# One plain feature tile fewer in each up product, and part of VectorE's preparation given to GpSimd

## The chip, the cores and the metric

The kernel runs on one core of a Trainium2 chip. A core has a matrix engine (TensorE, PE in the profile; PEld is its weight load), a vector engine (VectorE, DVE), an activation engine (ScalarE, ACT), a general engine (GpSimd, POOL) and a queue engine for transfers (SyncE, SP). Each runs its own instructions in order and waits for the others on semaphores. The metric is the device time of one launch in microseconds (us), here the median of several runs.

## The reference

One encoder layer over 512 tokens of 1024 channels, all in float32:

```python
def swiglu_ffn(x, w_gate, w_up, w_down):
    return (jax.nn.silu(x @ w_gate) * (x @ w_up)) @ w_down
...
x = x + 0.5 * swiglu_ffn(rmsnorm(x, ffn1_norm[l]), ffn1_w_gate[l], ffn1_w_up[l], ffn1_w_down[l])
x = x + hybrid_mixer(rmsnorm(x, mix_norm[l]), w_in[l], q_norm[l], k_norm[l], ...)
x = x + 0.5 * swiglu_ffn(rmsnorm(x, ffn2_norm[l]), ffn2_w_gate[l], ffn2_w_up[l], ffn2_w_down[l])
x = rmsnorm(x, final_norm[l])
```

The mixer (attention and pooling) lies between the two feed-forward blocks and isn't touched. A feed-forward block has 2816 features, 22 tiles of 128; each feature tile has a gate and an up column block.

## The kernel before, in words

**Numbers in two parts.** A float32 matmul operand is split into a high part (rounded by ScalarE) and a low part (the rest, a subtraction on VectorE, or a scaling and a subtraction). `split` does both, and `mm3` multiplies high by high, high by low and low by high: three matmuls for one product. So each operand, weights and activations, costs one ScalarE and one VectorE instruction before PE may use it.

**A plain feature tile.** Gate and up are each 8 blocks of 128 channels × 3 matmuls of 512 tokens, 48 matmuls. `evacuate` then multiplies the gate by the normalizer `norm.rb` (L424, from PSUM), applies SiLU on ScalarE (L426), multiplies by `norm.rb` again (L428) and has `down.place` multiply by the up product (L726, from PSUM). Every second tile is followed by two small operations on the stored result (L733, L734).

**A product tile.** The other feature tiles use a 2 × 2 block scheme with seven products in place of eight (Winograd's form): gate and up columns are the two columns of blocks of one operand, and channels and tokens are halved for the other. Seven products of 4 channel blocks × 3 matmuls of 256 tokens: 84 matmuls. The weight side needs per tile the parts of w11 (512 columns), the sums w13 and w24 (1024 each; L500, L506, L507) and w22 (1024), all with high parts at L477 and low parts at L482. The token side is made once for all product tiles, by `Norm.blocks`: eight scaled channel blocks (`scale`, L365), four sums of token blocks (`add`, L371: s1, s2, the sum in a21, s4), and seven split operands (L133 or L136): S2, S3, S4 as wholes of 1024 columns, and A11, A22, S1, A12 each as two halves of 512. In a product tile PE takes A11, S3, S2, A22, S1, A12, S4 in that order.

**The order.** `ffn_up` runs once for each feed-forward block. The first two feature tiles are multiplied together while the norm is finished; as soon as the normalizer is on the chip, the preparation by `Norm.blocks` may begin. Then come the remaining plain tiles, as many as `PLAIN` says for block 1 and block 2 (the two are counted in it), and the preparation is fed in between them by `piece`, from the list `todo`. The last plain tile also prepares the first product tile's weights. In the plain part a scheduler sets the order on each engine from its own estimates; only the transfers' queue keeps the order of the code. From the first product tile on the order of the code holds.

**GpSimd.** It issues the transfers that build sums of the down weights in memory (L717), a few after each feature tile, each group led by a one-column copy that holds it back (`mark`, L715); in the mixer it builds biases and trailing sums (L1221, L1430), and at the end of block 2 it multiplies by the last gain (L1808).

**Buffers.** Weight parts rotate through four places (three in `parts`, and `whi`/`wlo`). The halves `ha` take the buffers of the normalized input `hhi`/`hlo`, each free once PE's last plain tile has passed that channel block. `aside` holds the scaled blocks and sums.

Of the kernel before, what the change touches and what calls it, by code (L numbers as in the profile page):

```python
# [8 lines left out]
F32 = mybir.dt.float32  # L9
# [3 lines left out]
ALU = mybir.AluOpType  # L13
# [21 lines left out]
RAW = 2  # L35
HILO = 3
SHIFT = 16
PLAIN = (5, 4)
PROBS = 3
EARLY = 8  # L40
LATE = 12
# [15 lines left out]
def layer(  # L57
# [31 lines left out]
    nc = tc.nc  # L89
# [28 lines left out]
    A11, S1, S3, S2, A12, A22, S4 = range(7)  # L118
# [7 lines left out]
            what(*args)  # L126


    def split(src, hi, lo, scale=None):

        if scale is None:
            nc.scalar.copy(hi, src)  # L132
            nc.vector.tensor_tensor(lo, src, hi.bitcast(F32), op=ALU.subtract)  # L133
        else:
            nc.scalar.activation(hi, src, AF.Copy, scale=scale)
            nc.vector.scalar_tensor_tensor(  # L136
                lo, src, scale, hi.bitcast(F32), op0=ALU.mult, op1=ALU.subtract
            )
# [155 lines left out]
    class Norm:  # L294
# [5 lines left out]
        def add(self, k, square=True):  # L300
            hi = hpool.tile([P, S], F32R, tag="h", name=name("hhi"))
            lo = hpool.tile([P, S], F32R, tag="h", name=name("hlo"))
            split(x[k], hi, lo, gain_sb[:, self.which, k : k + 1])
            self.h[k] = hi, lo
            if square:
                self.square(k)
# [41 lines left out]
        def blocks(self, pool, aside):  # L348
# [7 lines left out]
            a11, a21 = x_lo[:, :, :HT], x_lo[:, :, HT:]  # L356
            a12, a22 = x_hi[:, :, :HT], x_hi[:, :, HT:]
            s2, s4, s1 = (
                z[:, at : at + 4 * HT].rearrange("p (k c) -> p k c", c=HT)
                for z, at in ((aside[0], 4 * S), (aside[1], 4 * S), (aside[2], 0))  # L360
            )
# [5 lines left out]
                    self.rb, op0=ALU.mult, op1=ALU.mult,  # L367
                )

            def add(dst, one, two, op):  # L370
                nc.vector.tensor_tensor(dst, one, two, op=op)  # L371

            def whole(i, src, make, sign=None):
                pair = [make().rearrange("p (k c) -> p k c", c=HT) for _ in range(2)]
                split(src, *pair, sign)
                self.a[i] = [[z[:, k] for k in range(4)] for z in pair]

            def halves(i, src):

                self.a[i] = [[], []]  # L380
                for k in (0, 2):
                    pair = [
                        hpool.tile([P, 2, HT], F32R, tag="h", name=name("ha")) for _ in range(2)
                    ]
                    split(src[:, k : k + 2], *pair)
                    for z, to in zip(pair, self.a[i]):
                        to.extend(z[:, j] for j in range(2))

            def by_x(i):
                return lambda: xpool.tile([P, 2 * S], F32R, tag=f"x{i.pop()}", name=name("xa"))  # L390

            def extra():
# [2 lines left out]

            free = [3, 2, 1, 0]
            return [(scale, k) for k in range(KD)] + [
                (add, s1, a21, a22, ALU.subtract),
                (add, s2, s1, a11, ALU.add),
                (add, a21, a11, a21, ALU.add),  # L400
                (whole, S3, a21, by_x(free), -1.0),
                (whole, S2, s2, by_x(free), -1.0),
                (add, s4, s2, a12, ALU.subtract),
                (whole, S4, s4, extra),
                (halves, A11, a11),
                (halves, A22, a22),
                (halves, S1, s1),
                (halves, A12, a12),
            ]


    def ffn_up(norm, wA, down, loaded, in_order, plain, turns=()):
# [9 lines left out]
        def evacuate(f, gate, up):  # L422
            g = temp()
            nc.vector.tensor_tensor(natural(g), ordered(gate), natural(norm.rb), op=ALU.mult)  # L424
            sg = temp()
            nc.scalar.activation(sg, g, AF.Silu)  # L426

            nc.vector.tensor_tensor(sg, sg, norm.rb, op=ALU.mult)  # L428
            down.place(f, ordered(up), sg)
            down.sums(f)  # L430
            return sg

        first = [bank() for _ in range(4)]
        for kp in range(KD // 2):
# [10 lines left out]
            for kk in range(2):  # L445
                k = 2 * kp + kk
# [1568 lines left out]
```

## Time and profile before

| what | value |
|---|---|
| median of 3 runs | 811.85 us (811.62 to 812.27) |
| the profiled execution | 811.69 us, span 809.7 us |
| PE busy | 797.8 us, 99% |
| VectorE busy | 712.8 us, 88% |
| ScalarE busy | 498.8 us, 62% |
| GpSimd busy | 147.2 us, 18% |
| mean granted clock of PE | 0.997 |

The span is counted from the first to the last instruction; the execution's own time holds about 2 us more around it. Times in the traces below start at the span's beginning. In a timeline row stand start, duration, engine, line, operation, out<-in and shape; idle time before it, and what ended it, in brackets. Neighbouring instructions of an engine overlap by some tens of nanoseconds, so what one costs its engine is read from start to start.

### The profile page before, as it was taken

How to read it: one execution, taken by the hardware profiler on the slowest of the kernel's cores; microseconds unless marked ns; L12 is line 12 of the kernel's file. 1: busy time of each engine (PE TensorE's matmuls, PEld its weight loads, DVE VectorE, ACT ScalarE, POOL GpSimd, SP SyncE). 2: the span in 40 equal slices, each digit the busy share in tenths (PEclk: the TensorE clock that was granted, in tenths of full speed). 3: DMA queues.
4: the chain of work that ended last, by engine and by line, in shares of the span. 5: the costliest groups of instructions: out<-in, count | busy, mean ns of one | idle time of the engine just before them, and what ended most of it. 6: DMA issues, size and time to landing. Idle time of an engine off the chain costs nothing.

```text
span 809.7 us, 14959 instructions
## 1 busy us (share of the span) xinstructions
PE 797.8 (99%) x5730; PEld 749.1 (93%) x5730; DVE 712.8 (88%) x1133; ACT 498.8 (62%) x854; POOL 147.2 (18%) x234
## 2 busy tenths in 40 slices
PE   9999999999999999999999999999999999999995
PEld 8889999999999999888888888899999999988985
DVE  7899999999996997778688788999999999987996
ACT  8446655556666665659659545465666655765683
POOL 0022212223220000100256354111111011100010
PEclk9999999999999999999999999999999999999998
DMA  8276889979999774431599777256666566969642
GB/s 289 76 208 208 237 226 247 216 189 249 248 292 316 220 219 147 142 124 34 156 258 248 196 198 210 80 112 204 172 184 151 163 185 168 272 210 344 211 120 104
DMA packets 73703, 158.56 MB, mean 196 GB/s; under 512 B 6544, under 2 KB 31648, under 8 KB 73248
## 3 DMA queue, kind: packets, MB, share of 16 engines
q1 hardware_dynamic: 49664, 109.09, 40.0%
q0 software_dynamic: 23680, 48.24, 28.3%
q8 instruction: 45, 0.74, 0.4%
q10 hardware_dynamic: 288, 0.27, 0.1%
q14 instruction: 26, 0.21, 0.1%
HBM read 153.38 MB, written 50.34 MB: 252 GB/s over the span
## 4 chain that ended last, share of the span: by engine, by line
PE 91%; DVE 4%; ACT 1%; issue 1%; DVEq 0%; ACTq 0%
PE mm L198 19%; PE mm L200 19%; PE mm L199 19%; PE a L199 10%; PE a L200 9%; PE a L198 9%; PE mm L1605 1%; PE mm L1516 1%; DVE aside L365 1%; PE a L1580 1%; PE mm L1580 1%; DVE aside L371 0%; PE a L1516 0%; DVE parts L133 0%; PE a L1605 0%
## 5 line engine op out<-in xcount | busy, mean ns | idle before, releaser
L571 ACT ACTIVATE t<-mm 128x256 f32<-128x256 f32 x105 | 40.5, 386 | 110.8 <-PE mm L200 108.8
L132 ACT CAST parts<-raw 128x1024 fp32r<-128x1024 f32 (+2 forms) x77 | 74.1, 968 | 54.7 <-PE mm L199 20.5
L133 DVE TENSOR_TENSOR parts<-raw,parts 128x1024 fp32r<-128x1024 f32 (+2 forms) x77 | 85.8, 1121 | 15.1 <-ACT parts L132 14.7
L199 PE MATMUL mm<-ha,parts 128*128 128x256 f32 x280 | 77.0, 275 | 0.0
L200 PE MATMUL mm<-ha,parts 128*128 128x256 f32 x280 | 77.0, 275 | 0.0
L198 PE MATMUL mm<-ha,parts 128*128 128x256 f32 x280 | 77.0, 275 | 0.0
L715 POOL COPY mark<-t 128x1 f32<-128x1 f32 x40 | 15.9, 397 | 330.9 <-DVE t L615 244.8
L717 POOL DMA_DIRECT2D wsum<-in_wB_dram x72 | 71.1, 1123 | 26.1 <-DMA wsum<-wsum 14.1
L482 DVE TENSOR_TENSOR parts<-wsum,parts 128x1024 fp32r<-128x1024 f32 x53 | 64.5, 1217 | 5.1 <-ACT parts L477 5.1
L477 ACT CAST parts<-wsum 128x1024 fp32r<-128x1024 f32 x53 | 53.9, 1047 | 0.6 <-PE mm L200 0.3
L198 PEld LDWEIGHTS mm<-ha,parts 128*128 128x128 f32 x280 | 53.8, 192 | 0.1
L199 PEld LDWEIGHTS mm<-ha,parts 128*128 128x128 f32 x280 | 53.8, 192 | 0.1
L200 PEld LDWEIGHTS mm<-ha,parts 128*128 128x128 f32 x280 | 53.8, 192 | 0.0
L198 PE MATMUL mm<-hhi,parts 128*128 128x512 f32 x128 | 49.6, 391 | 0.2
L200 PE MATMUL mm<-hhi,parts 128*128 128x512 f32 x128 | 48.7, 384 | 0.8 <-DVE parts L133 0.8
L133 DVE TENSOR_TENSOR ah<-acts,ah 128x512 fp32r<-128x512 f32 (+1 forms) x72 | 47.1, 662 | 2.7 <-ACT ah L132 2.4
L199 PE MATMUL mm<-hlo,parts 128*128 128x512 f32 x128 | 48.4, 379 | 0.0
L132 ACT CAST ah<-acts 128x512 fp32r<-128x512 f32 (+1 forms) x72 | 40.9, 580 | 8.8 <-PE mm L199 6.4
L482 DVE TENSOR_TENSOR parts<-raw,parts 128x512 fp32r<-128x512 f32 (+1 forms) x52 | 43.6, 858 | 0.5 <-ACT parts L477 0.5
L500 DVE TENSOR_TENSOR wsum<-raw 128x1024 f32<-128x1024 f32 x35 | 42.6, 1217 | 0.0
L477 ACT CAST parts<-raw 128x512 fp32r<-128x512 f32 (+1 forms) x52 | 39.2, 755 | 4.7 <-DMA raw<-in_wA_dram 3.4
L1122 DVE TENSOR_TENSOR parts<-raw,parts 128x1024 fp32r<-128x1024 f32 x24 | 30.1, 1258 | 11.6 <-ACT parts L1117 11.5
(342 smaller groups left out, 3062.0 us busy)
## 6 DMA issues: line engine op xcount, KB each, us to landing
raw<-in_wA_dram SPq DMA_DIRECT2D x87, 512.0 KB, 4.7
wsum<-in_wB_dram POOLq DMA_DIRECT2D x60, 512.0 KB, 7.5
raw<-wsum SPq DMA_DIRECT2D x36, 512.0 KB, 4.6
raw<-in_wB_dram SPq DMA_DIRECT2D x30, 512.0 KB, 4.9
wsum<-wsum POOLq DMA_DIRECT2D x20, 512.0 KB, 5.0
x<-in_xT_dram SPq DMA_DIRECT2D x16, 256.0 KB, 6.1
raw<-in_wQK_dram SPq DMA_DIRECT2D x8, 512.0 KB, 3.6
wsum<-in_wB_dram POOLq DMA_DIRECT2D x12, 256.0 KB, 5.5
```

The lines of the kernel that those rows point to most:

```text
L132: nc.scalar.copy(hi, src)
L133: nc.vector.tensor_tensor(lo, src, hi.bitcast(F32), op=ALU.subtract)
L198: nc.tensor.matmul(acc, a[0], high, start=start, stop=False, **more)
L199: nc.tensor.matmul(acc, a[0], low, start=False, stop=False, **more)
L200: nc.tensor.matmul(acc, a[1], high, start=False, stop=stop, **more)
L477: nc.scalar.copy(hi, src)
L482: nc.vector.tensor_tensor(lo, src, hi.bitcast(F32), op=ALU.subtract)
L500: nc.vector.tensor_tensor(z, raw[:, : 2 * S], raw[:, S : 3 * S], op=ALU.add)
L571: nc.scalar.activation(natural(dst), ordered(src), AF.Copy, scale=scale)
L717: nc.gpsimd.dma_start(self.rows(i, g), self.rows(self.terms[i][at], g), **(dict(accum_op=ALU.add) if at else {}),)
L1122: nc.vector.tensor_tensor(lo, buf["raw", i], hi.bitcast(F32), op=ALU.subtract)
L1580: nc.tensor.transpose(buf["tp", h, group][:, n : n + P], buf["p", h, t][:, j * P : (j + 1) * P], ident,)
```

## The change

`PLAIN` goes from (5, 4) to (4, 3): in each feed-forward block one feature tile fewer is multiplied plainly and one more as a product tile. Four kinds of VectorE work go to GpSimd: the second scaling in `evacuate` for all plain tiles, the sums a21 and s4 of `Norm.blocks`, and the low parts of S1 and A12. The list in `Norm.blocks` is written in another order.

```diff
-PLAIN = (5, 4)
+PLAIN = (4, 3)
...
-    def split(src, hi, lo, scale=None):
+    def split(src, hi, lo, scale=None, by=nc.vector):
...
-            nc.vector.tensor_tensor(lo, src, hi.bitcast(F32), op=ALU.subtract)
+            by.tensor_tensor(lo, src, hi.bitcast(F32), op=ALU.subtract)
...
-            def add(dst, one, two, op):
-                nc.vector.tensor_tensor(dst, one, two, op=op)
+            def add(by, dst, one, two, op):
+                by.tensor_tensor(dst, one, two, op=op)
...
-            def halves(i, src):
+            def halves(i, src, by=nc.vector):
...
-                    split(src[:, k : k + 2], *pair)
+                    split(src[:, k : k + 2], *pair, by=by)
...
             return [(scale, k) for k in range(KD)] + [
-                (add, s1, a21, a22, ALU.subtract),
-                (add, s2, s1, a11, ALU.add),
-                (add, a21, a11, a21, ALU.add),
+                (add, nc.vector, s1, a21, a22, ALU.subtract),
+                (add, nc.gpsimd, a21, a11, a21, ALU.add),
+                (add, nc.vector, s2, s1, a11, ALU.add),
+                (add, nc.gpsimd, s4, s2, a12, ALU.subtract),
+                (whole, S2, s2, by_x(free), -1.0),
                 (whole, S3, a21, by_x(free), -1.0),
-                (whole, S2, s2, by_x(free), -1.0),
-                (add, s4, s2, a12, ALU.subtract),
                 (whole, S4, s4, extra),
                 (halves, A11, a11),
                 (halves, A22, a22),
-                (halves, S1, s1),
-                (halves, A12, a12),
+                (halves, S1, s1, nc.gpsimd),
+                (halves, A12, a12, nc.gpsimd),
             ]
...
-            nc.vector.tensor_tensor(sg, sg, norm.rb, op=ALU.mult)
+            nc.gpsimd.tensor_tensor(sg, sg, norm.rb, op=ALU.mult)
```

How this moves instructions, in block 1. First GpSimd's queue before, from the first mark of block 1 on (`mark` is the one-column copy, `wsum` a sum of down weights):

```order
L715 COPY mark_114_471<-t_113_463 128x1
L717 DMA wsum_6_110<-in_wB1_dram 512x1x256
L717 DMA wsum_7_111<-in_wB1_dram 512x1x256
L715 COPY mark_133_570<-t_132_562 128x1
L717 DMA wsum_6_110<-in_wB1_dram 512x1x256
L717 DMA wsum_8_112<-in_wB1_dram 512x1x256
```

And the same place in the changed kernel, with what each row waits for (`t_102`, `t_104`, `t_113` are the SiLU results of the first three tiles, `aside_105` holds a21 and `aside_106` becomes s4, `ha_140` and `ha_142` are the low parts of S1, `ha_147` and `ha_149` those of A12, of which `ha_149` comes after the second group of transfers):

```order
L428 TENSOR_TENSOR t_102_380<-t_102_380,rb_100_352 128x512 [waits Activation_49]
L428 TENSOR_TENSOR t_104_386<-t_104_386,rb_100_352 128x512 [waits Activation_49]
L428 TENSOR_TENSOR t_113_463<-t_113_463,rb_100_352 128x512 [waits Activation_49]
L371 TENSOR_TENSOR aside_105_390<-aside_105_390 128x4x256 [waits DVE_49]
L715 COPY mark_114_471<-t_113_463 128x1 [waits Pool_49]
L717 DMA wsum_6_110<-in_wB1_dram 512x1x256
L717 DMA wsum_7_111<-in_wB1_dram 512x1x256
L371 TENSOR_TENSOR aside_106_391<-aside_105_390,aside_106_391 128x1024 [waits DVE_49]
L133 TENSOR_TENSOR ha_140_572<-aside_107_392,ha_139_571 128x512 [waits PE_49,Activation_49]
L133 TENSOR_TENSOR ha_142_576<-aside_107_392,ha_141_575 128x512 [waits PE_49,Activation_49]
L428 TENSOR_TENSOR t_144_595<-t_144_595,rb_100_352 128x512 [waits Activation_49]
L133 TENSOR_TENSOR ha_147_609<-aside_106_391,ha_146_608 128x512 [waits PE_49,Activation_49]
```

Nine computing instructions now stand in that queue ahead of or between the marks and transfers, ten with `ha_149`; before there was none.

Second, VectorE after the eight scalings, before (`t_112` is the third tile's gate; `aside_107` is s1; `wlo_121` the low part of the fourth tile's up weights; `xa` are S3 and S2):

```order
L424 TENSOR_TENSOR t_112_461<-mm_109_399,rb_100_352 128x512
L371 TENSOR_TENSOR aside_107_392<-aside_105_390,aside_106_391 128x1024
L428 TENSOR_TENSOR t_113_463<-t_113_463,rb_100_352 128x512
L371 TENSOR_TENSOR aside_105_390<-aside_107_392,aside_105_390 128x1024
L726 TENSOR_TENSOR acts_54_161<-mm_111_432,t_113_463 128x2x256
L371 TENSOR_TENSOR aside_105_390<-aside_105_390 128x4x256
L733 TENSOR_TENSOR acts_54_161<-acts_54_161 128x256
L133 TENSOR_TENSOR wlo_121_514<-raw_119_512,whi_120_513 128x1024
L734 TENSOR_TENSOR acts_54_161<-acts_54_161 128x256
L136 SCALAR_TENSOR_TENSOR xa_118_509<-aside_105_390,xa_117_508 128x1024
L136 SCALAR_TENSOR_TENSOR xa_124_544<-aside_105_390,xa_123_543 128x1024
L371 TENSOR_TENSOR aside_106_391<-aside_105_390,aside_106_391 128x1024
```

The same place now (`raw_127` holds the first product tile's weights, so the row of `parts_78` is w11's low part; `sa_120` is S4's low part, `ha_129` A11's first):

```order
L424 TENSOR_TENSOR t_112_461<-mm_109_399,rb_100_352 128x512
L371 TENSOR_TENSOR aside_107_392<-aside_105_390,aside_106_391 128x1024
L133 TENSOR_TENSOR wlo_124_498<-raw_122_496,whi_123_497 128x1024
L371 TENSOR_TENSOR aside_105_390<-aside_107_392,aside_105_390 128x1024
L136 SCALAR_TENSOR_TENSOR xa_118_485<-aside_105_390,xa_117_484 128x1024
L726 TENSOR_TENSOR acts_54_161<-mm_111_432,t_113_463 128x2x256
L136 SCALAR_TENSOR_TENSOR xa_116_481<-aside_105_390,xa_115_480 128x1024
L733 TENSOR_TENSOR acts_54_161<-acts_54_161 128x256
L482 TENSOR_TENSOR parts_78<-raw_127_504,parts_78 128x512
L734 TENSOR_TENSOR acts_54_161<-acts_54_161 128x256
L133 TENSOR_TENSOR sa_120_489<-aside_106_391,sa_119_488 128x1024
L133 TENSOR_TENSOR ha_129_522<-aside_105_390,ha_128_521 128x512
```

The fourth tile's other weights are gone, the two sums and the second scalings have left the list, and the preparation of the first product tile has moved up behind the third tile; S3's and S4's low parts now stand behind sums that GpSimd makes.

Third, PE in the first product tile, from the product with S1 to the one with S4. In the kernel before none of its rows waits for GpSimd. Now (every third row or so is shown; `ha_139` to `ha_142` are S1, `ha_146` to `ha_149` A12, `sa` S4):

```order
L198 MATMUL mm_153_621<-ha_139_571,parts_78 128x256 [waits Activation_49]
L199 MATMUL mm_153_621<-ha_140_572,parts_78 128x256 [waits Pool_49]
...
L199 MATMUL mm_153_621<-ha_142_576,parts_78 128x256 [waits Pool_49]
...
L199 MATMUL mm_154_622<-ha_147_609,whi_159_639 128x256 [waits Pool_49]
...
L199 MATMUL mm_154_622<-ha_149_613,whi_159_639 128x256 [waits Pool_49]
...
L198 MATMUL mm_153_621<-sa_119_488,whi_159_639 128x256 [waits Activation_49]
```

Four waits of PE now end with GpSimd.

## The prediction

> **What bounds the kernel now.** I read the page first, then the waits of PE, then the timeline engine by engine around the plain tiles of both feed-forward blocks, then busy time by stretch.
>
> ```profile
> span 809.7 us, 14959 instructions
> PE 797.8 (99%) x5730; PEld 749.1 (93%) x5730; DVE 712.8 (88%) x1133; ACT 498.8 (62%) x854; POOL 147.2 (18%) x234
> ...
> PE mm L200 <- DVE parts L133: 0.8, 1, 0.8
> ...
> 29.21 0.38 PE L198 MATMUL mm<-hhi,parts 128*128 128x512 f32 x1
> 39.57 0.38 PE L198 MATMUL mm<-hhi,parts 128*128 128x512 f32 x1
> 61.33 0.27 PE L198 MATMUL mm<-ha,parts 128*128 128x256 f32 x1
> 71.10 0.28 PE L198 MATMUL mm<-ha,parts 128*128 128x256 f32 x1
> 541.33 0.28 PE L198 MATMUL mm<-ha,parts 128*128 128x256 f32 x1
> ...
> 155.20 0.42 ACT L628 ACTIVATE t<-t 128x256 f32<-128x256 f32 x1
> 202.10 0.42 ACT L628 ACTIVATE t<-t 128x256 f32<-128x256 f32 x1
> ...
> core 0: us, PE busy (x) PEld busy (x) DVE busy (x) ACT busy (x) POOL busy (x), PEclk, DMA share, GB/s
> 28.30:63.67 35.37, 34.60 (x171) 30.24 (x170) 35.32 (x48) 17.19 (x23) 5.76 (x6) 1.00 0.41 119
> 499.06:533.46 34.40, 34.31 (x167) 29.95 (x166) 33.09 (x44) 16.12 (x22) 6.67 (x7) 1.00 0.32 99
> ```
>
> PE is the bound, and nearly without waits. But the second-last row says more: from the moment that the normalizer is there (28.30) until the low part of the first product tile's w24 is made (63.67), DVE is busy 35.32 of 35.37 us. There PE and DVE are two chains of equal length, and the one wait of PE in that stretch (0.8 us) is for DVE. GpSimd is nearly empty there.
>
> **The change part by part.**
>
> *A plain tile becomes a product tile, twice.* A plain tile takes PE 39.57 − 29.21 = 10.36 us (48 matmuls). A product tile takes (202.10 − 155.20) / 5 = 9.38 us: five tiles lie between those two rows (84 matmuls, 0.112 us each). Gain 0.98 us a tile, 1.96 us in both blocks, 0.24% of the time. That is all the change can win on PE. 0.2% (1.6 us) is about what a measurement of this kernel can tell from no change.
>
> *But PE reaches the product tiles 10.36 us earlier, and DVE must have their operands ready.* Prices on DVE, start to start:
>
> ```profile
> 28.30 0.69 DVE L424 TENSOR_TENSOR t<-mm,rb 128x512 f32<-128x512 f32 x1 [2.10 <-ACT rb L342]
> 28.91 0.74 DVE L365 SCALAR_TENSOR_TENSOR aside<-x,gain_sb,rb 128x512 f32<-128x512 f32 x1
> 29.57 0.68 DVE L424 TENSOR_TENSOR t<-mm,rb 128x512 f32<-128x512 f32 x1
> ...
> 41.28 1.22 DVE L371 TENSOR_TENSOR aside<-aside 128x1024 f32<-128x1024 f32 x1
> 42.41 0.42 DVE L733 TENSOR_TENSOR acts<-acts 128x256 f32<-128x256 f32 x1
> 42.75 1.22 DVE L133 TENSOR_TENSOR wlo<-raw,whi 128x1024 fp32r<-128x1024 f32 x1
> ...
> 62.53 1.21 DVE L482 TENSOR_TENSOR parts<-wsum,parts 128x1024 fp32r<-128x1024 f32 x1
> ```
>
> So 0.60 us for 512 columns, 0.66 for a scaling (L365), 1.13 for 1024, 0.34 for 256. In the new order DVE has these from its first L424 to the low part of w24 in block 1: 14 of 512 (four L424, three L726, four halves, three weight rows), 8 scalings, 10 of 1024, 2 of 256: 8.4 + 5.3 + 11.3 + 0.7 = 25.7 us against 35.4 before. Alone, DVE would end w24 at 28.30 + 25.7 = 54.0. PE wants it (third matmul of product S2) at 29.21 + 2 × 10.36 + 26 × 0.112 = 52.8. So even with GpSimd free of cost there is a match within 1.2 us and no room.
>
> *What moves to GpSimd:* in block 1 four second scalings (L428), the additions a21 and s4, and four low parts (S1, A12). Its prices, and what they do to DVE:
>
> ```profile
> 435.00 1.07 POOL L1430 TENSOR_TENSOR us<-u 128x527 f32<-128x527 f32 x1 [1.25 <-DVE sm L1540]
> ...
> 774.47 0.68 DVE L1789 SCALAR_TENSOR_TENSOR xt<-mm,xt 128x512 f32<-128x512 f32 x1
> 774.88 1.28 POOL L1808 TENSOR_TENSOR xt<-xt,t 128x512 f32<-128x512 f32 x1 [73.70 <-ACT t L1804]
> 775.40 1.30 DVE L133 TENSOR_TENSOR ah<-acts,ah 128x512 fp32r<-128x512 f32 x1
> 778.70 1.21 DVE L133 TENSOR_TENSOR parts<-raw,parts 128x1024 fp32r<-128x1024 f32 x1
> 779.07 1.98 POOL L1808 TENSOR_TENSOR xt<-xt,t 128x512 f32<-128x512 f32 x1 [2.92 <-ACT t L1804]
> 779.83 1.50 DVE L133 TENSOR_TENSOR ah<-acts,ah 128x256 fp32r<-128x256 f32 x1
> ...
> 520.16 1.21 DVE L133 TENSOR_TENSOR wlo<-raw,whi 128x1024 fp32r<-128x1024 f32 x1
> 520.37 2.79 POOL L715 COPY mark<-t 128x1 f32<-128x1 f32 x1 [18.24 <-DVE t L428]
> 523.04 0.68 DVE L726 TENSOR_TENSOR acts<-mm,t 128x512 f32<-128x512 f32 x1
> 98.09 0.24 POOL L715 COPY mark<-t 128x1 f32<-128x1 f32 x1 [8.05 <-DVE t L615]
> ```
>
> A GpSimd operation over 512 columns takes 1.07 to 1.28 us, twice DVE's price; for 1024 columns I double it: 2.1 to 2.5. And the two engines exclude each other. DVE's 512 columns at 775.40 take 1.30 instead of 0.68 and end only 0.5 us after GpSimd's; its 256 columns at 779.83 take 1.50 instead of 0.42, held by the GpSimd operation, which itself took 1.98 because DVE was busy when it came. A one-column copy, 0.24 us otherwise, took 2.79 at 520.37 and ended when DVE came to L726. DVE's L726, L424 and L1789 read PSUM and one SBUF operand and don't collide; nearly all else here reads two SBUF operands. So the moved work leaves DVE's list but not DVE's time: each operation costs DVE up to its full 1.07 to 1.28, less what falls beside an L424 or L726 (0.6).
>
> Who gets the turn isn't settled by the rows: at 779.07 GpSimd waited for one operation of DVE, at 520.37 through several. The Trainium skill (SBUF — State Buffer, Who interferes with whom) says that the pair of ports is an exclusive lock which the operation that starts first holds to its end. The first row agrees; the wait at 520.37 is longer than that rule alone gives. By the rule, turn by turn with no overlap and no late A12, the two blocks would lose 10.2 + 7.0 = 17.2 us; by the long wait, with all overlap and A12 late, 4.1 + 2.6 + 12 = 18.7 (terms below).
>
> *Block 1.* Before w24's low part GpSimd does three L428, a21, s4 and the two low parts of S1: 5 × (1.07 to 1.28) + 2 × (2.1 to 2.5) = 9.5 to 11.4 us. At best 4.2 us of that fall beside the seven PSUM operations (7 × 0.6), at worst none: w24 at 59.3 to 65.4. I take the middle, 62.4, as the rows show both an overlap (774.88) and none (779.07). From there PE needs 6.5 us to end the tile (58 matmuls) and 9.38 for the added one: 78.3, where before it stood at 71.10. Loss 7.2 (4.1 to 10.2).
>
> *A12's low parts.* These are last in GpSimd's queue, behind the fourth L428, a mark and two DMA issues:
>
> ```profile
> 52.30 1.97 POOL L717 DMA_DIRECT2D wsum<-in_wB_dram  x2
> ```
>
> That is 3 × (1.07 to 1.28) + 0.24 + 1.97 = 5.4 to 6.0 us after S1's, and PE wants the last one 4.5 us after w24. If S1's were done well before w24 nothing waits; if after, up to 6. I take 3.
>
> *Block 2.* Rows as before:
>
> ```profile
> 499.06 2.73 DVE L365 SCALAR_TENSOR_TENSOR aside<-x,gain_sb,rb 128x512 f32<-128x512 f32 x4
> 511.27 0.38 PE L199 MATMUL mm<-hlo,parts 128*128 128x512 f32 x1
> ```
>
> DVE's list from 499.06 to w24's low part: 8 scalings, 10 of 1024, 12 of 512, 2 of 256 = 24.5 us, ending 523.6 alone. PE's third tile starts one matmul before that row, at 511.05, and ends, plain, at 511.05 + 10.36 = 521.4 and wants w24 at 524.3. GpSimd's part by then: two L428, a21, s4, one S1 half = 7.4 to 8.8, less 0 to 3.0 beside five PSUM operations: 528.0 to 532.4, middle 530.2. With 6.5 + 9.38: 546.1 against 541.33 before: loss 4.8 (2.6 to 7.0), and 3 (0 to 6) again for A12. Here a21 also queues behind two L428 that can't start before their L424 of about 512; DVE's list covers that.
>
> *Clock.* Waits of this size may cost clock.
>
> ```profile
> 801.25 0.28 PE L200 MATMUL a<-parts,ah 128*128 128x256 f32 x1
> 801.00:805.00 4.00, 0.52 (x5) 0.33 (x3) 3.37 (x17) 2.48 (x7) 0.73 (x2) 0.96 0.00 0
> 805.00:809.00 4.00, 0.00 (x0) 0.00 (x0) 0.50 (x2) 0.47 (x1) 0.00 (x0) 0.50 0.68 262
> ```
>
> After the last matmul (ended 801.53) the granted clock falls to 0.50; a mean of 0.96 puts that at 804.7, 3.2 us later. PE's waits above come in pieces of 3 to 4 us. If a return takes as long as the fall, one drop costs 1.6 us, and two 3.2; the trace shows no return, so 0 to 3.2, and I take 1.6. The Trainium skill (TensorE: Matmul & The Clock Gate, What's actually happening) puts the window at 3.4 us for both directions, 1.7 us a drop, and nothing if no wait fills a window.
>
> *Costed at nothing:* ACT (17.19 of 35.37 us busy); the transfers for the sums on GpSimd's queue, which issue a few us later and are first read at the end of the product tiles, 17 × 9.38 us on (without that cover each us late would be one for PE); the reordering of S3 before S2 on DVE, which the sums contain.
>
> *Sum:* 7.2 + 3 + 4.8 + 3 + 1.6 = 19.6, with the 1.96 already inside (the ends were compared tile for tile). The profiled execution took 811.69, 0.16 below the median: 811.85 + 19.6, about 831.
>
> **Rivals.**
>
> *The ports hardly matter and the cover holds (not slower).* DVE's list ends at 54.0 and 523.6, GpSimd's runs beside it. Then block 1 gains 0.98 − 1.2, block 2 0.98: 811.1; if GpSimd's own latency (a21 before S3's high part) makes DVE wait some 2 us, 813. It decides where the collisions cost under 0.5 us a block. Against it: 775.40, 779.83 and 520.37, all collisions found where a GpSimd operation that reads SBUF met a busy DVE.
>
> *Only block 1 pays.* In block 2 DVE alone is 0.7 us ahead of PE and has gaps (33.09 busy of 34.40). If GpSimd fits there, 811.85 + 7.2 + 3 − 0.98 = 821. Against it: after the change those gaps shrink with the 10.36 us.
>
> *DVE keeps its turn throughout, and A12 comes last.* GpSimd gets in only beside L424 and L726 or when DVE itself waits for it: upper ends, 10.2 + 6 + 7.0 + 6 + 3.2 = 32: 844. For it: 520.37. Against it: 779.07.
>
> **How the numbers follow.** Both blocks pay, 824 to 838: 0.66. Only block 1, 818 to 823: 0.17. DVE keeps its turn, 839 to 845: 0.06. No price, 809.9 to 813.5: 0.11, of which faster 0.05, same 0.05, slower 0.01. The range runs from 817 (a little below the lower ends, 811.85 + 4.1 + 2.6 = 818.6) to 843 and leaves out about 0.15. Faster 0.05, same 0.05, slower 0.90; time 831.
>
> **What would show it.** Right: DVE's L133, L371 and L365 between the normalizer and the first product tile longer than 0.68, 1.22 and 0.74 where GpSimd runs; L428 and the moved L133 on GpSimd well over 1.28 us; PE waiting 5 us or more a block, for DVE at w13 or w24 and for GpSimd's `ha`; product tiles after that still 9.38. Wrong: GpSimd's L428 at 1.1 to 1.3 with DVE's rows unchanged, and PE at its first product within 2 us of 49.9. I would also be wrong if the waits at 520.37 and 779.07 had another cause than DVE, or if PE made up the loss later, where it is 99% busy.

## The result, and the profile after

The changed kernel takes 842.9 us (median of 4 runs, 842.29 to 843.13); the kernel before took 812.06 on the same chip (811.62 to 812.61). The ratio is 1.0379 (95% interval 1.0364 to 1.0395): 30.8 us slower; the forecast was 831, 19 more than before.

The page of the changed kernel, its first lines, and then what PE waited for (engine, line, who ended the wait: us in total, times, longest):

```profile
span 841.0 us, 15135 instructions
PE 807.9 (96%) x5802; PEld 758.5 (90%) x5802; DVE 727.4 (86%) x1126; ACT 503.8 (60%) x868; POOL 180.9 (22%) x253
```

```profile
PE mm L199 <- DVE parts L1122: 7.0, 1, 7.0
PE mm L199 <- DVE ha L133: 4.9, 1, 4.9
PE mm L200 <- DVE parts L482: 3.8, 2, 2.5
PE mm L198 <- DVE acts L726: 3.2, 1, 3.2
```

PE was 99% busy and is 96%. The longest wait is at a line the prediction doesn't speak of: L1122 makes the low parts of the mixer's weights, between the two feed-forward blocks.

To place the loss I take landmarks of the timelines. L636 is ACT's last SiLU of a product tile; the last one of a block closes its up product. L342 copies a normalizer, the second one at the end of the mixer. First the kernel before, then the changed one:

```profile
222.27 0.38 ACT L636 ACTIVATE t<-mm 128x256 f32<-128x256 f32 x1
497.11 0.59 ACT L342 COPY rb<-a 128x512 f32<-128x512 f32 x1 [0.33 <-PE a L340]
701.89 0.38 ACT L636 ACTIVATE t<-mm 128x256 f32<-128x256 f32 x1
```

```profile
83.94 0.39 ACT L636 ACTIVATE t<-mm 128x256 f32<-128x256 f32 x1
234.93 0.38 ACT L636 ACTIVATE t<-mm 128x256 f32<-128x256 f32 x1
520.06 0.59 ACT L342 COPY rb<-a 128x512 f32<-128x512 f32 x1 [0.52 <-PE a L340]
733.17 0.38 ACT L636 ACTIVATE t<-mm 128x256 f32<-128x256 f32 x1
```

So block 1's up product ends 12.7 us later, the mixer 23.0 later, block 2's up product 31.3 later; behind it nothing is added (VectorE's last sum of the output starts at 836.04 against 804.75). Three places lost: block 1 12.7, the mixer 10.3, block 2 8.3. Busy time by stretch says the same (PE, PEld, DVE, ACT, POOL busy with their counts, then granted clock, DMA share, GB/s):

```profile
28.30:63.67 35.37, 28.81 (x129) 24.68 (x127) 29.72 (x34) 14.79 (x23) 17.88 (x10) 0.86 0.18 61
60.00:70.00 10.00, 7.61 (x35) 7.02 (x34) 8.80 (x8) 4.07 (x9) 10.00 (x8) 0.50 0.35 107
90.00:240.00 150.00, 150.00 (x1346) 150.00 (x1345) 140.62 (x199) 92.75 (x164) 39.26 (x56) 1.00 0.90 231
333.00:343.00 10.00, 4.38 (x39) 4.08 (x37) 6.42 (x12) 6.62 (x10) 0.00 (x0) 0.86 0.15 35
```

From 90 to 240 PE is busy without a gap: nothing is lost among the later product tiles. Around block 1's first product tile, PE is idle for 6.6 of 35.4 us and then runs at half clock (0.50 from 60 to 70); at the mixer's start it is idle for 5.6 of 10.

**Block 1.** Rows of GpSimd, VectorE, ACT and PE of the changed kernel:

```profile
39.20 3.80 POOL L428 TENSOR_TENSOR t<-t,rb 128x512 f32<-128x512 f32 x1 [6.47 <-ACT t L426]
42.96 2.36 POOL L371 TENSOR_TENSOR aside<-aside 128x1024 f32<-128x1024 f32 x1
...
46.85 2.60 POOL L371 TENSOR_TENSOR aside<-aside,aside 128x1024 f32<-128x1024 f32 x1
...
40.64 1.21 DVE L371 TENSOR_TENSOR aside<-aside,aside 128x1024 f32<-128x1024 f32 x1
46.45 4.10 DVE L136 SCALAR_TENSOR_TENSOR xa<-aside,xa 128x1024 fp32r<-128x1024 f32 x1 [4.59 <-ACT xa L135]
...
62.74 2.32 DVE L482 TENSOR_TENSOR parts<-wsum,parts 128x1024 fp32r<-128x1024 f32 x1
...
45.35 2.01 ACT L135 ACTIVATE xa<-aside 128x1024 fp32r<-128x1024 f32 x2 [6.23 <-POOL aside L371]
...
55.34 0.58 PE L199 MATMUL mm<-ha,parts 128*128 128x256 f32 x1 [4.90 <-DVE ha L133]
65.11 0.58 PE L200 MATMUL mm<-xa,parts 128*128 128x256 f32 x1 [1.29 <-DVE parts L482]
```

Read it as one chain. GpSimd's third second scaling (L428) comes at 39.20 and takes 3.80 us in place of 1.28: it ends at 43.00, 1.15 us after VectorE's row of 40.64 (41.85). Behind it on GpSimd's queue stands the sum a21 (42.96), and on its end ACT waits for S3 (L135, 6.23 us idle). VectorE, in order, waits for ACT, and then stands 4.10 us in L136, which ends 1.10 us after GpSimd's s4 (49.45). From the end of its L371 (41.85) to the end of L136 (50.55) VectorE does one operation of 1.13 us: a hole of 7.6 us in the engine that PE waits for. w24's low part ends at 65.06. From VectorE's first L424 (28.55) that is 36.5 us, 10.8 more than the 25.7 of its list alone, and 7.6 of them are the hole.

**The mixer's start.** ACT's first high part of mixer weights, before and after, and PE after:

```profile
317.75 1.05 ACT L1117 CAST parts<-raw 128x1024 fp32r<-128x1024 f32 x1 [1.43 <-PE a L199]
```

```profile
335.75 1.05 ACT L1117 CAST parts<-raw 128x1024 fp32r<-128x1024 f32 x1 [7.32 <-PE a L199]
344.34 0.79 PE L199 MATMUL mm<-parts,hhi 128*128 128x512 f32 x1 [6.96 <-DVE parts L1122]
```

Behind block 1 everything is 12.7 us late, yet this row is 18.0 late: ACT waits for a matmul of the last down products to let a buffer go.

**Block 2**, where the two engines took turns:

```profile
539.07 9.02 DVE L133 TENSOR_TENSOR ha<-aside,ha 128x512 fp32r<-128x512 f32 x4
...
553.97 2.28 DVE L482 TENSOR_TENSOR parts<-wsum,parts 128x1024 fp32r<-128x1024 f32 x1
...
548.84 0.55 PE L198 MATMUL mm<-ha,parts 128*128 128x256 f32 x1 [3.20 <-DVE acts L726]
556.30 0.38 PE L200 MATMUL mm<-xa,parts 128*128 128x256 f32 x1 [2.49 <-DVE parts L482]
```

Four of VectorE's halves, 2.4 us in the kernel before, took 9.02 beside GpSimd's two sums and its two low parts of S1 (538.03 to 547.55).

### The profile page after: what moved, and what is told of

It reads as the page before. It is cut to its first block, busy times and chain, and to the rows that moved or that the text cites. A ratio compares the mean times of both kernels' runs of the same rounds, so it can differ in the third digit from the quotient of the medians.

```text
span 841.0 us, 15135 instructions
## 1 busy us (share of the span) xinstructions
PE 807.9 (96%) x5802; PEld 758.5 (90%) x5802; DVE 727.4 (86%) x1126; ACT 503.8 (60%) x868; POOL 180.9 (22%) x253
## 4 chain that ended last, share of the span: by engine, by line
PE 85%; DVE 7%; ACT 1%; issue 1%; POOL 1%; DMA 1%; SPq 0%; DVEq 0%; ACTq 0%
PE mm L198 18%; PE mm L200 18%; PE mm L199 18%; PE a L200 9%; PE a L198 9%; PE a L199 9%; DVE ha L133 1%; DVE xa L136 1%; DMA raw<-wsum 1%; DVE parts L482 1%; PE mm L1605 1%; PE mm L1516 1%; DVE aside L365 1%; POOL t L428 1%; PE a L1580 0%
## 5 line engine op out<-in xcount | busy, mean ns | idle before, releaser
L482 DVE TENSOR_TENSOR parts<-wsum,parts 128x1024 fp32r<-128x1024 f32 x74 | 93.5, 1263 | 9.5 <-ACT parts L477 9.3
L133 DVE TENSOR_TENSOR parts<-raw,parts 128x1024 fp32r<-128x1024 f32 (+2 forms) x75 | 83.9, 1124 | 15.2 <-ACT parts L132 14.8
L199 PE MATMUL mm<-ha,parts 128*128 128x256 f32 x296 | 83.0, 281 | 5.0 <-DVE ha L133 4.9
L198 PE MATMUL mm<-ha,parts 128*128 128x256 f32 x296 | 82.7, 279 | 3.2 <-DVE acts L726 3.2
L200 PE MATMUL mm<-ha,parts 128*128 128x256 f32 x296 | 82.6, 279 | 0.0
L477 ACT CAST parts<-wsum 128x1024 fp32r<-128x1024 f32 x74 | 74.0, 1044 | 7.5 <-DVE wsum L500 5.7
L715 POOL COPY mark<-t 128x1 f32<-128x1 f32 x40 | 11.7, 292 | 263.9 <-DVE t L615 263.9
L199 PEld LDWEIGHTS mm<-ha,parts 128*128 128x128 f32 x296 | 58.0, 196 | 5.6 <-DVE ha L133 5.6
L198 PEld LDWEIGHTS mm<-ha,parts 128*128 128x128 f32 x296 | 58.0, 196 | 3.6 <-issue 3.6
L200 PEld LDWEIGHTS mm<-ha,parts 128*128 128x128 f32 x296 | 58.1, 196 | 0.0
L133 DVE TENSOR_TENSOR ah<-acts,ah 128x512 fp32r<-128x512 f32 (+1 forms) x72 | 47.8, 671 | 3.2 <-ACT ah L132 2.9
L482 DVE TENSOR_TENSOR wlo<-raw,whi 128x1024 fp32r<-128x1024 f32 x37 | 47.1, 1273 | 0.0
L200 PE MATMUL mm<-xa,parts 128*128 128x256 f32 x148 | 41.7, 282 | 3.8 <-DVE parts L482 3.8
L500 DVE TENSOR_TENSOR wsum<-raw 128x1024 f32<-128x1024 f32 x37 | 45.1, 1218 | 0.0
L1117 ACT CAST parts<-raw 128x1024 fp32r<-128x1024 f32 x24 | 25.1, 1045 | 29.7 <-PE a L199 10.0
L198 PE MATMUL mm<-xa,parts 128*128 128x256 f32 x148 | 41.6, 281 | 1.1 <-ACT t L571 1.1
L1122 DVE TENSOR_TENSOR parts<-raw,parts 128x1024 fp32r<-128x1024 f32 x24 | 29.6, 1240 | 14.9 <-ACT parts L1117 14.8
L200 PE MATMUL a<-xa,parts 128*128 128x256 f32 x148 | 41.5, 281 | 0.5 <-DVE parts L482 0.5
```

Source lines behind the costliest of these rows:

```text
L133: by.tensor_tensor(lo, src, hi.bitcast(F32), op=ALU.subtract)
L198: nc.tensor.matmul(acc, a[0], high, start=start, stop=False, **more)
L199: nc.tensor.matmul(acc, a[0], low, start=False, stop=False, **more)
L200: nc.tensor.matmul(acc, a[1], high, start=False, stop=stop, **more)
L500: nc.vector.tensor_tensor(z, raw[:, : 2 * S], raw[:, S : 3 * S], op=ALU.add)
L1117: return lambda: nc.scalar.copy(buf["part", i][0], buf["raw", i])
```

## The experiments

Twelve runs. The table has each kernel's loss against the median of the kernel before on the same chip, and where it arose by the landmarks (block 1's last L636, then the second L342, then block 2's last L636):

| kernel | loss, us | ratio (95% interval) | block 1 | mixer | block 2 |
|---|---|---|---|---|---|
| the change | 30.8 | 1.0379 (1.0364 to 1.0395) | 12.7 | 10.3 | 8.3 |
| change, places set right | 23.0 | 1.0279 (1.0262 to 1.0296) | 13.1 | 0.2 | 9.6 |
| before, places shifted | 11.1 | 1.0136 (1.0121 to 1.0151) | 0.2 | 9.1 | 1.3 |
| tile alone | 9.3 | 1.0116 (1.0101 to 1.0131) | 6.5 | −0.5 | 2.7 |
| moves alone | 18.5 | 1.0226 (1.0211 to 1.0242) | 14.9 | −0.1 | 3.8 |
| second scaling alone | 10.4 | 1.0127 (1.0107 to 1.0147) | 10.1 | −1.1 | 3.4 |
| sums alone | 8.2 | 1.0099 (1.0084 to 1.0114) | 5.1 | 0.1 | 1.2 |
| low parts alone | 3.6 | 1.0042 (1.0026 to 1.0059) | 2.7 | −0.1 | 0.5 |
| an added scaling | 5.6 | 1.0069 (1.0054 to 1.0084) | 2.4 | −0.7 | 3.3 |
| places right, sums back | 12.9 | 1.0162 (1.0148 to 1.0176) | 10.7 | −0.1 | 3.8 |
| places right, scaling back | 18.7 | 1.0224 (1.0203 to 1.0245) | 13.1 | −0.1 | 7.3 |
| places right, low parts back | 18.6 | 1.0227 (1.0213 to 1.0241) | 12.2 | −0.5 | 5.6 |

The places are read from one profiled execution of each kernel, which can lie up to 2.1 us from the median beside it. The twelfth run, with added matmuls, is told at the end.

**The places of the weight parts.** `part_tiles` hands out four places in turn. A plain tile calls it twice, a product tile four times, so block 1 now makes 8 + 18 × 4 = 80 calls ahead of the 77 down products, not 10 + 17 × 4 = 78. In the kernel before the last three down products hold places 0, 1, 2 in this order; now the last holds place 0, and the mixer takes place 0 first. Both kernels were run with the count started at 2:

```diff
-    n_parts = [0]
+    n_parts = [2]
-    n_own = [0]
+    n_own = [2]
```

> The changed kernel, with the rotation of the four weight-part places started two calls later, so that the calls of block 1 end on the same place as in the kernel before (a plain tile makes two calls, a product tile four; 78 calls before block 1's down products became 80). Theory A (places): the mixer's first weights go to place 0, which the very last down product holds now and the third last held before; moved back, the 10.2 us at the start of the mixer come back: 832 to 834, PE without its 7.0 us wait for L1122, and the other two losses (12.6 in block 1, 8.3 in block 2) as they are. Rival B (late start: the mixer's weights are late because everything ahead is late, or the clock is): 842 to 844, the wait stays.

> The kernel before, with nothing changed but the start of the rotation by two calls, so that its last down product holds place 0 as in the changed kernel. Theory A: 10 us slower, 821 to 823, all of it between the last down products and the mixer's first projections (PE waits some 7 us for L1122). Rival B: 811.5 to 812.5, no wait there.

Measured: 834.57 and 822.74. The kernel before, with no other edit, shows the very wait of the change:

```profile
PE mm L199 <- DVE parts L1122: 7.0, 1, 7.0
```

In the changed kernel it is gone, and the mixer's 10.3 us with it. Theory A holds both ways. The first run lies 0.6 above its range, and by the landmarks it is block 2 that loses more (9.6 in place of 8.3; 1.3 in the kernel before). The start of the count shifts the places there too, and the work stands in another order: PE's longest wait is 4.48 us for L136, in place of 3.20 for L726. No run separates the two.

**The tile alone, the moves alone.** `tile_only` is the kernel before with `PLAIN = (4, 3)` and the count started at 2; `moves_only` is the changed kernel with `PLAIN = (5, 4)`:

```diff
-PLAIN = (4, 3)
+PLAIN = (5, 4)
```

> The kernel before with one plain tile less in each block and nothing on GpSimd or reordered; the rotation is started two calls later, so that the mixer's start is as before. VectorE's list in block 1 is one tile shorter (two low parts of weights 2 x 1.13, L424, L428, L726 3 x 0.60: 4.1 us), so w24's low part comes at 63.7 - 4.1 = 59.6 and the first product tile ends at 59.6 + 6.5 + 9.4 = 75.5, 4.4 after the kernel before; in block 2 533.5 - 4.1 + 15.9 = 545.3 at most, or 2.7 less where its gaps close: 1.3 to 4.0 late. Theory C (GpSimd's operations exclude VectorE's and so cost more than they take off VectorE): 817 to 821, that is 12 to 15 us faster than the same kernel with the moves. Rival D (the tile's removal is the loss, the moves help or are neutral): 832 or more.

> The kernel before, with as many plain tiles as before, but the moved operations on GpSimd and the new order of the sums. VectorE's list in block 1 is 7.1 us shorter (9 rows of 512 columns at 0.60 and 2 sums at 1.13, less the fifth L428 that adds a GpSimd operation). Theory C: five or more GpSimd operations ahead of w24 give back 10 to 12 us less up to 5 that fall beside PSUM operations: w24 at 63 to 70 where it was at 62.5, A12's low parts up to 6 late, block 2 0 to 3: 813 to 824. Rival D: 811 to 812.5, PE's waits not above 1.5 us in either block.

Measured: 820.93 and 830.14. The tile's removal costs 9.3 us with VectorE doing everything; the moves make that 23.0, and alone cost 18.5, 6 us above the upper end I gave them. They relieve nothing. In `tile_only` VectorE has no gap up to w24's low part, and PE waits at the last plain tile and at the first product tile:

```profile
47.77 0.48 PE L200 MATMUL mm<-hhi,parts 128*128 128x512 f32 x1 [2.31 <-DVE parts L133]
58.05 0.58 PE L198 MATMUL mm<-xa,parts 128*128 128x256 f32 x1 [2.48 <-ACT t L571]
```

Part of the 14.9 in `moves_only` is a cost that the whole change doesn't show, a late transfer (ACT and PE, second product tile):

```profile
85.97 0.62 ACT L477 CAST parts<-raw 128x512 fp32r<-128x512 f32 x1 [4.88 <-DMA raw<-in_wA_dram]
...
86.92 0.58 PE L198 MATMUL a<-ha,parts 128*128 128x256 f32 x1 [4.07 <-ACT t L571]
```

The load of these weights was issued at 75.36, behind the late first product tile, and took 10.6 us to land; the same load before was issued at 66.49 and took 6.0. GpSimd's sum transfers, issued from 73.39 to 78.79, were under way beside it; that they held it is likely, but no run shows it. In block 1 ACT's wait of this kind is 4.13 us in the run with the scaling alone, 2.89 in the one with the low parts alone, and 3.73 and 2.23 in two of the last three runs below.

**The exclusion by itself.** Nothing is moved; GpSimd makes a second copy of each plain tile's second scaling into a tile that is not read:

```diff
             nc.vector.tensor_tensor(sg, sg, norm.rb, op=ALU.mult)
+            nc.gpsimd.tensor_tensor(down.junk, sg, norm.rb, op=ALU.mult)
```

> The kernel before, nothing moved; GpSimd only does a second copy of each plain tile's second scaling into a tile that nobody reads (five operations over 512 columns in block 1, four in block 2), behind VectorE's own. VectorE's list and every chain of operands stay as they were, so whatever is lost is the exclusion alone. Theory C (GpSimd's operation holds off VectorE's two-operand operations while it runs): three or four of them lie in block 1 ahead of the first product tile's w24, up to 1.28 us each less what falls beside L424 or L726, and VectorE had no slack there: 1 to 5 us a block, 813 to 820. Rival E (only the chains through GpSimd cost, not the exclusion): 811.2 to 812.5.

Measured: 817.09; theory C. GpSimd and VectorE of this kernel (its lines from 429 on are one or two higher):

```profile
40.70 2.13 POOL L429 TENSOR_TENSOR junk<-t,rb 128x512 f32<-128x512 f32 x1 [5.68 <-DVE t L428]
...
42.21 1.71 DVE L371 TENSOR_TENSOR aside<-aside 128x1024 f32<-128x1024 f32 x1
...
64.31 1.21 DVE L483 TENSOR_TENSOR parts<-wsum,parts 128x1024 fp32r<-128x1024 f32 x1
```

w24's low part comes at 64.31 where it came at 62.53. Four GpSimd operations lie ahead of it: 0.45 us of VectorE's time for each, not 1.07 to 1.28. VectorE has an operation that reads PSUM beside each of them (0.60 us), and one row behind that grows by 0.4 to 0.5, as L371 at 42.21 does from 1.22 to 1.71. In block 2 three of them make w24 1.3 us late. The exclusion is real and small: 1.8 us in block 1, where the moves alone lose 14.9. The 5.6 of the whole kernel are not the exclusion alone: in block 2 PE waits another 1.7 us behind a late transfer.

**The three moves one by one,** each put alone on the kernel before:

```diff
-            nc.vector.tensor_tensor(sg, sg, norm.rb, op=ALU.mult)
+            nc.gpsimd.tensor_tensor(sg, sg, norm.rb, op=ALU.mult)
```

> The kernel before, with L428 alone on GpSimd. VectorE's list loses 0.60 for each, 2.4 us ahead of w24. Theory C: each costs VectorE up to 1.28 again and waits for its turn up to 3.8 us, L726 and the bank of the tile's up half follow it: a loss of 0 to 5 in both blocks together, 811 to 817. Rival E: a gain or nothing, 810.5 to 812.5, as nothing behind L726 is near PE.

```diff
+                (add, nc.gpsimd, a21, a11, a21, ALU.add),
+                (add, nc.gpsimd, s4, s2, a12, ALU.subtract),
```

> The kernel before, with the two additions a21 and s4 alone on GpSimd and the order of the change. In the run with all moves VectorE stood 4.59 us idle and then 2.9 us held at L136 behind these two additions, and this is the largest piece of its 14.9 us in block 1. Theory F (the hole is the additions' own: GpSimd takes 2.36 us for each, must find a gap in VectorE's row of L365, and ACT and VectorE wait for its result): 6 to 10 us in block 1, 0 to 3 in block 2, 818 to 825. Rival G (the hole came from the starved L428 that stood ahead of them in GpSimd's queue): below 5 us in all, 811.5 to 816.5.

```diff
+                (halves, S1, s1, nc.gpsimd),
+                (halves, A12, a12, nc.gpsimd),
```

> The kernel before, with the low parts of S1 and A12 alone on GpSimd. VectorE's list loses 2.4 us, four GpSimd operations of 1.28 to 1.95 us come in the 10 us ahead of the first product tile's products S1 and A12. Theory C: A12's late by up to 6 us, w24 held by up to 2.5: 1 to 6 in block 1, 0 to 3 in block 2, 812 to 819. Rival E: 811 to 812.5. If the three parts are independent, this and the two others add up to the 18.5 us of all moves together; if one is queued behind another on GpSimd, they add up to clearly less.

Measured: 821.88, 819.66, 815.09. The scaling alone costs twice the upper end I gave it; the low parts alone lie where theory C put them. GpSimd, then VectorE, of that run:

```profile
39.34 4.95 POOL L428 TENSOR_TENSOR t<-t,rb 128x512 f32<-128x512 f32 x1 [6.47 <-ACT t L426]
...
44.32 0.69 DVE L726 TENSOR_TENSOR acts<-mm,t 128x512 f32<-128x512 f32 x1 [1.19 <-POOL t L428]
```

Here GpSimd gets in only when VectorE pauses: L428 ends at 44.29, one undisturbed 1.28 us behind the end of VectorE's row before the pause (43.14), and that pause is VectorE's wait for L428. In the sums' run a hole like that of the change appears without any starved L428 ahead of it:

```profile
38.90 3.88 POOL L371 TENSOR_TENSOR aside<-aside 128x1024 f32<-128x1024 f32 x1 [37.10 <-DVE aside L371]
...
45.30 2.62 POOL L371 TENSOR_TENSOR aside<-aside,aside 128x1024 f32<-128x1024 f32 x1
...
40.46 0.68 DVE L726 TENSOR_TENSOR acts<-mm,t 128x512 f32<-128x512 f32 x1
41.06 2.80 DVE L133 TENSOR_TENSOR wlo<-raw,whi 128x1024 fp32r<-128x1024 f32 x1
...
44.12 4.89 DVE L136 SCALAR_TENSOR_TENSOR xa<-aside,xa 128x1024 fp32r<-128x1024 f32 x1
```

VectorE is not idle in it: it stands in two rows, L133 and L136, together 5.4 us longer than their 1.13 each. ACT converts S2 first in this run (40.58), so VectorE need not wait for a21 as in the change. The total is theory F's, though block 1 loses 5.1, less than the 6 to 10 it gave. The list of the change, in its new order, goes with the sums in this run, and no run has that order alone. The three add up to 22.1, more than the 18.5 of all at once: not independent, and not queued up behind each other either. That they share stalls would explain it, and is not shown; two of them have a late transfer.

**The three moves taken back,** each from the changed kernel with its places right (834.57): the diffs above, reversed, and for the sums the old order of the list.

> The changed kernel with its weight-part places set right (the run at 834.6 us), and the two additions a21 and s4 and their order given back to VectorE; the scalings and the low parts stay on GpSimd. Theory F (VectorE's and ACT's wait for these additions is the largest single piece): 6 to 10 us come back, 824 to 829. Rival G (they only hand on the delay of the starved L428 ahead of them): 2 us or less, 832 to 835.

> The changed kernel with its places set right, and only the second scaling L428 given back to VectorE. Theory G (the starved L428 of 3.80 us stands ahead of a21 on GpSimd's queue): a21 starts some 4 us earlier and 4 to 9 us come back, 825 to 831. Theory F: 0 to 3 us, since a21 must then find its own gap between VectorE's operations, 831 to 835.

> The changed kernel with its places set right, and only the low parts of S1 and A12 given back to VectorE. Theory C (each costs VectorE about what it takes off it, and alone in the kernel before they lost 3.6 us): 1 to 4 us come back, 830.5 to 833.5. Rival H (with VectorE the last to be ready, they do relieve it): 0 to 3 us slower, 834.5 to 838.

Measured: 825.19, 830.98, 830.90. By the losses, each against the kernel before on its own chip, the sums give back 10.0 us, the scaling 4.2, the low parts 4.3. Theory F holds: the sums, with their order, are the costliest move. The scaling's result lies on the border of G and F, and decides nothing; its profiled execution also has a late transfer (PE waits 2.4 us for it at 87.94) that the run it is compared with does not have. The low parts don't relieve VectorE either (C). With the sums back GpSimd is still held off: its third L428 takes 4.95 us, and three low parts of S1 and A12 take 7.45 together, where 3.8 is their price. GpSimd, then VectorE:

```profile
39.40 4.95 POOL L428 TENSOR_TENSOR t<-t,rb 128x512 f32<-128x512 f32 x1 [6.47 <-ACT t L426]
...
54.90 7.45 POOL L133 TENSOR_TENSOR ha<-aside,ha 128x512 fp32r<-128x512 f32 x3 [8.69 <-ACT ha L132]
...
39.71 1.21 DVE L133 TENSOR_TENSOR parts<-raw,parts 128x1024 fp32r<-128x1024 f32 x1
41.98 1.21 DVE L371 TENSOR_TENSOR aside<-aside 128x1024 f32<-128x1024 f32 x1
```

**The half clock.** In the run with the places right, PE's wait before w24 ends at 64.78. From there PE is busy, at 0.21 us a matmul, and the first at 0.11 is that of 68.13, 3.35 us later:

```profile
64.78 0.58 PE L200 MATMUL mm<-xa,parts 128*128 128x256 f32 x1 [1.58 <-DVE parts L482]
...
68.13 0.27 PE L200 MATMUL a<-ha,parts 128*128 128x256 f32 x1
```

Added matmuls were to keep the clock up:

```diff
+                warm(n, 40 if plain == PLAIN[0] else 20, up_lo, w11)
                 product(acc, w11, A11, True)
...
+        def warm(n, times, to, w):
+            if n == plain:
+                for _ in range(times):
+                    nc.tensor.matmul(to, w[0][:, :P], w[0][:, :HT], start=True, stop=True)
```

(and the same with 40 ahead of S2 in block 1 and ahead of S3 in block 2)

> The changed kernel with its places set right, and added matmuls of 128x256 with no one to read them in the first product tile of each block, where PE waits: 40 ahead of A11 and 40 ahead of S2 in block 1, 20 ahead of A11 and 40 ahead of S3 in block 2 (0.11 us each at full clock). Theory K (the half clock after the waits costs): in block 1 the 16 matmuls after the last wait (64.78) took 0.21 instead of 0.11, 1.6 us; in block 2 those from 545 to 548 as much again or up to 3: 830 to 832.5. Rival L (the operands come when VectorE and GpSimd have them, and the clock is back before it matters): 833.5 to 836.

Measured: 834.91, ratio to the kernel before 1.0283 (1.0269 to 1.0297), the number of rival L. But the run doesn't settle it. Its clock from 65 to 70 was 1.00, where it was 0.69 without the added matmuls; yet those held PE until 66.66, past 64.78, though w24's low part was there (its row ends at 64.75):

```profile
65.00:70.00 5.00, 5.00 (x46) 5.00 (x45) 4.00 (x4) 0.39 (x1) 5.00 (x6) 1.00 0.50 156
```

```profile
66.66 0.28 PE L198 MATMUL mm<-xa,parts 128*128 128x256 f32 x1
```

The time says that what the clock gave, the matmuls that bought it took. Whether a shorter filling pays stays open.

No run beats the kernel before. Block 1's VectorE list was as long as PE's, and no single move to GpSimd made w24's low part ready sooner: it ends at 65.7, 68.4 and 63.8 with the scaling, the sums or the low parts moved, and at 63.7 before.

## Why the prediction was right and wrong

The direction was right, and in the two feed-forward blocks the sum was near (19.6 against 21.0), but with terms that were off both ways, as this table shows; 10.3 us came from a place that the sum didn't have. That the time (842.9) still lies in the range of 817 to 843 is luck: in the two blocks the terms' errors cancelled, and the mixer's loss filled what the range had kept for late low parts of A12 and for the clock.

| term | predicted | measured |
|---|---|---|
| block 1, w24's low part | 7.2 (4.1 to 10.2) | 9.9 |
| block 2, w24's low part | 4.8 (2.6 to 7.0) | 7.9 |
| A12's low parts, both blocks | 6 (0 to 12) | 0 |
| clock, both blocks | 1.6 (0 to 3.2) | 2.7 |
| second product tile beyond 9.38 | none | 0.4 |
| mixer's start | none | 10.3 |

- **w24's low part** ended at 65.06, against 62.4 (59.3 to 65.4): 2.7 late, 7.2 + 2.7. In block 2 it ended at 556.25; less the 23.0 by which the block began late, 533.25 against 530.2, 0.9 beyond the upper end. Right in kind, mis-sized, and in part for the wrong reason: the step "each operation costs DVE up to its full 1.07 to 1.28" is 0.45 in the run with the added scaling. What it left out is that VectorE stands still for a result that GpSimd could not begin: the hole of 7.6 us.
- **"The reordering of S3 before S2 on DVE, which the sums contain"** was costed at nothing. S3's conversion stands first on ACT and on VectorE, so S2, ready at 41.85, waited behind GpSimd's a21 with it; in the kernel before ACT converted S2 first, at 40.79, while VectorE's a21 was still to come (41.28). The sums, taken back with their order, give back most (10.0); how much of that is the order's, no run shows.
- **A12's low parts**: PE has no wait after 65.11 in block 1 or after 556.30 in block 2. PE itself was late enough to cover them: in block 1 the last of them ends at 70.96, and PE's product A12 begins at 71.59. The waits for GpSimd's `ha` that the prediction named as a sign never came.
- **Clock**: after 65.11 PE had 58 matmuls to the end of the tile, 6.5 us at full clock, and took 9.2, 2.7 more: up to 70.59 they came every 0.21 us, with a granted clock of 0.50 from 60 to 70. The term took a return of 3.2 us, and this one took 5.5. In block 2 the same 58, from 556.30, took 6.6, so nothing was lost there. The first matmul of the next tile in each block:

```profile
74.27 0.28 PE L198 MATMUL mm<-ha,parts 128*128 128x256 f32 x1
562.88 0.28 PE L198 MATMUL mm<-ha,parts 128*128 128x256 f32 x1
```

  The second product tile took 9.47 and 9.73 us (to 83.74 and 572.61), together 0.4 more than twice 9.38. The terms then come to 20.9; the landmarks say 21.0.
- **"The transfers for the sums"**, costed at nothing: nothing in the change itself (PE is full from 90 to 240), but in block 1 of five runs with parts of it ACT waits 2.2 to 4.9 us for a late weight transfer. That GpSimd's transfers held it is likely, and not shown.
- **The gain of 1.96** is inside these differences: the later product tiles come as they did, 16 of them in 150.99 us (83.94 to 234.93) and 150.97 before (71.30 to 222.27). It is the one thing that was read off without an assumption.
- **The failing step** is one that the prediction doesn't have: that a product tile draws four weight parts and a plain tile two, so that the change moves the places of every later weight. I counted what the change moved on the engines, not what it moved in the rotation of buffers. "If PE made up the loss later, where it is 99% busy" was named as a way to be wrong; that it could lose more there was not.
- **The rivals.** That the ports hardly matter is refuted as a forecast, though the collisions by themselves are cheap (0.45 each, 1.8 in block 1, more than the 0.5 it needed). That only block 1 pays is refuted by block 2's 8.3. The third rival's time, 844, is the nearest to the one measured, but not its mechanism: A12 came last and cost nothing, and GpSimd was not kept out throughout (block 2 shows turns).

The tile's removal was the smaller mistake of the change. By itself it made VectorE's list 4.1 us shorter for 10.36 us less time, and cost 9.3; the moves that were to pay for it cost 13.7 more (23.0 − 9.3).

## What to carry to other kernels

Before work is moved to an engine that shares a resource with a busy one, look who waits for the result: 0.45 us of collision became a hole of 7.6, because the helper could not begin until the busy engine paused, and the busy engine paused only to wait for the helper. When a change alters how many buffers a stage draws, count on to the end of the rotation and see who takes over the last place: here two calls more cost 10 us, in a stage that the change does not touch. An engine without slack is relieved by less work, not by work that it must wait for.

## What the hardware showed that I had not expected

- Which engine gets the shared access was, by the starts of the rows, not settled by the order of arrival. GpSimd's L428 in the run with the sums back came at 39.40 and ended at 44.35: one undisturbed 1.28 us behind the end of VectorE's operation of 41.98 (41.98 + 1.13 = 43.11), though that one and the one at 39.71 began after it. The Trainium skill (SBUF — State Buffer, Who interferes with whom) says that whoever starts first has the pair for its whole instruction; the trace agrees on the whole instruction, and not on the first.
- It got in beside an operation that reads PSUM: the sum at 38.90 ended at 42.78, 2.32 after VectorE's L726 at 40.46; 2.36 is what the sum at 42.96 took in the changed kernel, with VectorE idle.
- VectorE can be held from ahead as well: its L136 at 44.12 in the run with the sums alone began 1.2 us before the row of GpSimd's second sum (45.30) and still took 4.89. GpSimd was issuing two transfers when it began; with the sums back an L136 at 44.99 took 1.22 beside the same two issues (from 44.53), so these alone do not hold it. How much of the 4.89 is the access, and how much another wait inside the row, no run shows.
- How long PE has to be busy until the granted clock comes back is not one number. From the end of a wait to the first matmul at full speed it took 3.25 us in block 2 of the change (548.84 to 552.09), 3.35 in the run with the places right (64.78 to 68.13), but 5.5 in block 1 of the change (65.11 to 70.59), 6.1 at its mixer's start (344.34 to 350.46) and 6.3 in `tile_only` (58.05 to 64.34). The Trainium skill (TensorE: Matmul & The Clock Gate, What's actually happening) gives a window of about 3.4 us for the return; the two short rows agree with it, the three long ones do not. The trace of before showed only the fall.
